# A hand-written opening in another order, and a full 128-row sample chunk in the HGRN tail

## The chip, the core and the metric

The kernel runs on one core of a Trainium2 chip, in one launch. The metric is the device time of that core in microseconds (us), the median of several runs; smaller is better. A core has five engines that each take their instructions strictly in order: TensorE (PE, matmuls; its weight loads are shown apart as PEld), VectorE (DVE), ScalarE (ACT), GpSimd (POOL), and SyncE (SP), which here only issues the transfers (DMA). They wait for each other through semaphores.

## What is computed

One inference step of one layer: 2048 new tokens of one stream (the prompt) and 64 tokens of a running stream (the sample), 1024 columns each, in float32.

```python
h = rms_norm(x, norm_g);  proj = h @ w_in                     # 6656 columns
hg_q, hg_f, hg_i, hg_gate, rt_q, rt_k, rt_v, rt_gate, xa_q, xa_gate = split(proj)
o_hg, s_hg = hgrn2_chunkwise(silu(hg_q), (1-lb)*sigmoid(-hg_f), hg_i, log f, state)   # 8 heads of 128
o_rt, s_rt = retention_chunkwise(rope(rt_q), rope(rt_k), rt_v, state)                 # 4 heads
m = rms_norm(mem, mem_norm_g);  mk, mv = m @ w_mem_k, m @ w_mem_v                      # 256 memory rows
o_xa = softmax(xa_q @ mk.T) @ mv                                                       # 4 heads
mixed = concat(norm(o_hg)*silu(hg_gate), norm(o_rt)*silu(rt_gate), o_xa*silu(xa_gate))
y = rms_norm(x + mixed @ w_out)                                # and the new states, mk and mv are outputs
```

The sample uses its own memory keys and values and its own states.

## The kernel before

**Matmuls.** Every large product is made of three matmuls in a 32-bit format of PE: each operand is split into a high part (ACT casts, L240 `split`, L379) and a low part (DVE subtracts, L241, L381), and hi*hi, lo*hi and hi*lo are summed in one PSUM bank. `gemm_col` (L243) makes 128 columns of a projection for one tile of tokens: 8 steps of the 1024 rows with 3 matmuls each, 24 in all. `gemm_pair` (L258) makes two such columns at once, step by step in turn, 48 matmuls.

**Weights.** All weights go through one list (`wsrc`) of 0.5 MB pieces in the order of their use: 4 pieces of `w_mk`, 4 of `w_mv`, then `w_in` and `w_out`. A piece is loaded to one of three staging tiles (`wst`), split to one of six pairs `whi`, `wlo`, and its staging tile is free again when DVE's part is done; only then can SP issue the load that reuses it. `w_rel` gives credit for the next split.

**Order.** PE's and SP's orders, and in the opening also those of ACT, DVE and POOL, are those of the code (`manual_schedule`). SP's transfers rotate over eight completion semaphores, so a transfer also waits for the eighth one ahead of it. After the opening, short tasks (`task`, `poll`) are put between the columns' steps at times that a running sum of estimated PE time (`pe`) sets; the `D_` constants are their delays.

**The opening.** From the start on:
- The memory (256 rows, transposed) is scaled and split to `mh` (L882 on ACT, L883 on DVE). POOL squares and sums it (L885, L887).
- The four memory-key heads (`gemm_col` on `mh`), then the memory values from four weight pieces of 256 rows (L942, called mv here).
- The row scales: squares summed over the 1024 columns, a matmul with ones (`rs_tok`, L335), DVE's scale and offset (L342) and POOL's power -0.5 (L343). To use them along the free axis, they are put on a diagonal (`rs_diag`, L349), broadcast by a matmul with ones (`rs_bcast`, L357) and copied by ACT (L361). This is done for the memory, for tile 0 (tokens 0 to 511) and tile 1 (512 to 1023).
- `h_split` then scales each of the eight row groups of a tile (L378) and splits it to `ha` (tile 0) or `hb` (tile 1). Between the steps of tile 0, `sq1` squares tile 1 on ACT and sums it on POOL (L929, L931).
- `gemm_pair` of the first two retention-gate columns for tile 0 (PE, 43 to 63 us), two more columns, and the same for tile 1.

**The HGRN tail.** Tokens come in chunks of 128; the last tile (1792, 320 tokens) has two prompt chunks and the sample's 64 rows. For each of 8 heads and each tile, `hgrn_tail` transposes the keys (L526), makes the scores as matmuls of 32 output rows each (L533), masks them (L538), makes the state products (L542), the outputs from scores and from state (L574, L577), squares and normalises them (L582, L236, L237, L586) and transposes them back (L593). The sample's chunk has L = 64: its steps use 64 rows, and `parts` splits the shared steps in two.

## Time and profile before

| | |
|---|---|
| median of 3 runs | 1966.73 us (1966.49 to 1967.02) |
| the profiled execution: its time | 1968.01 us |
| its span (first to last instruction) | 1966.2 us |
| PE busy | 1924.1 us, 98% |
| DVE, ACT, POOL busy | 1049.2, 584.6, 163.9 us |
| mean granted PE clock | 0.992 |
| transfers | 153.19 MB, mean 78 GB/s |

In the rows of this document a line number (L249) is that of the kernel's file, an arrow reads "out from in", xN is a count, and a row in order of time begins with its start and its length in us; what stands in brackets is the idle time of the engine before it and what ended that. Names are those of the code without buffer numbers. [...]

### The profile page before, as it was taken

The page shows a single profiled execution, that of the slowest core. Times are in us where ns is not written, and L with a number is a line of the kernel's source. Part 1 is how long each engine was busy: PE and PEld are TensorE (multiplying, and loading weights), DVE is VectorE, ACT ScalarE, POOL GpSimd, SP SyncE. Part 2 cuts the span into 40 slices and gives each one's busy share as a digit, 9 for nine tenths or more (in the row PEclk, how much of TensorE's full clock was granted, in tenths as well). Part 3 has the DMA queues.
Part 4 walks back from the last instruction along what each step waited for, and adds up shares of the span by engine and source line. Part 5 has one row for each costly group of instructions (what it writes and reads, how often), then busy time and mean ns, then how long its engine had stood idle before and what let it go on. Part 6 is the DMA issues. An engine that isn't in the chain of part 4 may idle for free.

```text
span 1966.2 us, 28106 instructions
## 1 busy us (share of the span) xinstructions
PE 1924.1 (98%) x10906; PEld 1624.0 (83%) x10906; DVE 1049.2 (53%) x2511; ACT 584.6 (30%) x1418; POOL 163.9 (8%) x363
## 2 busy tenths in 40 slices
PE   8999999999999999999999999999999999999998
PEld 7788788888888788987788888888888978888886
DVE  7616647762767547417637775477765642222222
ACT  5522223322223534412323332233334431111111
POOL 3100101000100100000101111021100000000000
PEclk8999999999999999999999999999999999999999
DMA  7422311111111423311311111111222352223321
GB/s 251 146 67 63 87 50 48 60 54 49 44 44 60 130 75 121 124 53 53 91 46 49 49 49 48 43 49 49 59 70 70 106 160 86 86 89 109 102 70 59
DMA packets 116741, 153.19 MB, mean 78 GB/s; under 512 B 13312, under 2 KB 79232, under 8 KB 116608
## 3 DMA queue, kind: packets, MB, share of 16 engines
q1 hardware_dynamic: 116608, 151.41, 25.2%
q8 instruction: 85, 1.39, 0.3%
q14 instruction: 48, 0.39, 0.1%
HBM read 117.69 MB, written 33.69 MB: 77 GB/s over the span
## 4 chain that ended last, share of the span: by engine, by line
PE 87%; DVE 6%; DMA 3%; ACT 2%; issue 1%; POOL 1%; SPq 0%; DVEq 0%; POOLq 0%; ACTq 0%
PE acc L249 39%; PE acc L1131 19%; PE acc L294 15%; PE scb L533 2%; PE ob L542 2%; PE ob L574 2%; PE ob L577 1%; PE acc L806 1%; PE ob L762 1%; DVE wlo L241 1%; PE acc L264 1%; PE tr L593 1%; PE tr L526 1%; PE tr L784 1%; DMA wst<-w_mv_t 1%
## 5 line engine op out<-in xcount | busy, mean ns | idle before, releaser
L249 PE MATMUL acc<-hb,whi 128*128 128x320 f32 (+2 forms) x1728 | 414.6, 330 | 0.4 <-DVE hb L381 0.4
L249 PE MATMUL acc<-ha,whi 128*128 128x512 f32 x1120 | 354.6, 398 | 0.0
L249 PEld LDWEIGHTS acc<-hb,whi 128*128 128x128 f32 x1728 | 289.3, 189 | 25.0 <-issue 4.4
L241 DVE TENSOR_TENSOR wlo<-wst,whi 128x1024 fp32r<-128x1024 f32 x118 | 146.0, 1246 | 273.4 <-ACT whi L240 272.4
L249 PE MATMUL acc<-hb,wlo 128*128 128x320 f32 (+2 forms) x864 | 281.3, 326 | 0.0
L249 PEld LDWEIGHTS acc<-ha,whi 128*128 128x128 f32 x1120 | 204.3, 188 | 42.9 <-issue 2.4
L249 PE MATMUL acc<-ha,wlo 128*128 128x512 f32 x560 | 219.4, 392 | 0.0
L240 ACT CAST whi<-wst 128x1024 fp32r<-128x1024 f32 x118 | 122.9, 1050 | 225.4 <-PE acc L249 172.1
L249 PEld LDWEIGHTS acc<-hb,wlo 128*128 128x128 f32 x864 | 163.1, 189 | 11.1
L294 PE MATMUL acc<-whi,ha 128*128 128x512 f32 x512 | 161.2, 396 | 0.0
L294 PE MATMUL acc<-whi,hb 128*128 128x512 f32 x512 | 160.1, 394 | 0.0
L1131 PE MATMUL acc<-whi,s 128*128 128x512 f32 x396 | 125.9, 396 | 1.3 <-ACT s L240 1.0
L249 PEld LDWEIGHTS acc<-ha,wlo 128*128 128x128 f32 x560 | 105.4, 188 | 23.1
L294 PEld LDWEIGHTS acc<-whi,hb 128*128 128x128 f32 x512 | 94.5, 188 | 19.9 <-issue 1.2
L294 PEld LDWEIGHTS acc<-whi,ha 128*128 128x128 f32 x512 | 93.8, 188 | 19.9 <-issue 1.2
L294 PE MATMUL acc<-wlo,ha 128*128 128x512 f32 x256 | 100.1, 391 | 0.0
L294 PE MATMUL acc<-wlo,hb 128*128 128x512 f32 x256 | 99.8, 390 | 0.0
L1131 PE MATMUL acc<-hb,s 128*128 128x512 f32 x400 | 98.5, 403 | 0.0
L1131 PE MATMUL acc<-ha,s 128*128 128x512 f32 x400 | 96.4, 396 | 0.0
L1131 PEld LDWEIGHTS acc<-hb,s 128*128 128x128 f32 x400 | 76.9, 192 | 18.7
L241 DVE TENSOR_TENSOR s<-mst,s 128x512 fp32r<-128x512 f32 (+1 forms) x64 | 40.5, 672 | 96.4 <-ACT s L240 96.4
L1131 PEld LDWEIGHTS acc<-whi,s 128*128 128x128 f32 x396 | 74.3, 188 | 19.6 <-ACT s L240 1.3
(236 smaller groups left out, 2932.0 us busy)
## 6 DMA issues: line engine op xcount, KB each, us to landing
wst<-w_in_t SPq DMA_DIRECT2D x104, 512.0 KB, 3.9
mixT<-s SPq DMA_DIRECT2D x64, 256.0 KB, 3.7
mst<-mixT SPq DMA_DIRECT2D x30, 512.0 KB, 6.0
wst<-w_out_t SPq DMA_DIRECT2D x16, 512.0 KB, 3.9
xq<-x_prompt SPq DMA_DIRECT2D x18, 256.0 KB, 5.4
o_yp<-xq SPq DMA_DIRECT2D x18, 256.0 KB, 2.1
s<-mixT SPq DMA_DIRECT2D x16, 256.0 KB, 3.0
s<-x_prompt SPq DMA_DIRECT2D x16, 256.0 KB, 5.0
```

The lines of the kernel that those rows point to most:

```text
L240: S.copy(hi, src)
L241: V.tensor_tensor(out=lo, in0=src, in1=hi.bitcast(F32), op=ALU.subtract)
L249: T.matmul(ps[:, 0:nt], w[a][:, kk, :], ht[b][:, kk, 0:nt], start=(n == 0), stop=(n == 23))
L264: T.matmul(ps[:, 0:nt], w[a][:, kk, :], ht[b][:, kk, 0:nt], start=(kk == 0 and a + b == 0), stop=(kk == KT - 1 and a == 1))
L294: T.matmul(ps[0:L, :], ht[b][:, kk, o:o + L], w[a][:, kk % 2, :], start=(n == 0), stop=(n == 23))
L526: T.transpose(trk[0:L, c * 128:(c + 1) * 128], kch[:, c * 128:c * 128 + L], ident)
L533: T.matmul(scb[32 * e:32 * e + 32, c * 128 + 32 * e:c * 128 + L], K[:, c * 128 + 32 * e:c * 128 + 32 * e + 32], Qe[:, c, E_OFF[e]:E_OFF[e] ...
L542: T.matmul(db[:, c * 128:(c + 1) * 128], kT[0:L, c * 128:(c + 1) * 128], vt[c][0:L], start=True, stop=True)
L574: T.matmul(ob[0:L, c * 128:(c + 1) * 128], A[0:L, c * 128:c * 128 + L], vt[c][0:L], start=True, stop=first)
L577: T.matmul(ob[0:L, c * 128:(c + 1) * 128], qst[:, c * 128:c * 128 + L], st[c][0], start=False, stop=True)
L593: T.transpose(tro[:, o:o + L], on[0:L, c * 128:(c + 1) * 128], ident[0:L, 0:L])
L1131: T.matmul(ps, m[a][:, kk % 4], w[b], start=(n == 0), stop=(n == 16 * len(terms) - 1))
```

## The change

It has two parts. The changed file's line numbers are lower or higher by some tens: L516, L522, L531, L563, L566 and L581 are there what L526, L533, L542, L574, L577 and L593 are here, L368 and L371 are L378 and L381, L896 and L897 are L882 and L883, L933 is L942, and L858 is the new sum of squares.

1. **The opening is written in another order.** SP issues the memory ahead of all but the first weight piece, and tile 0 before the value weights. The squares of the memory are made by ACT and all sums by DVE (`add_tree`), also those of tiles 0 and 1; POOL keeps the power. ACT makes the squares of tile 0 before the memory-key heads end. The row scale of tile 0 is made right after these heads. The memory-key results stay in two PSUM banks; their scale, their stores and the mask are made by a task (`mk_fin`) some 24 us of PE time later. One value-weight quarter of the four is done at a time between the other steps, the last two after the broadcast. Tile 1's sums are made after tile 0's splits, and its scale is delayed further (`D_PQ1`, `D_PR1`).
2. **The sample's chunk in `hgrn_tail` has 128 rows**, the lower 64 being zero or masked: POOL fills the lower half of its value tile with zeros, the score matmuls go over four groups of 32 rows instead of two, and the steps split by `parts` are one step each.

On POOL, at the start of its work (in both, behind the fills of constants; `rsall` are the row scales, `s` working tiles). Before:

```order
L885 ISA
L885 TENSOR_TENSOR s<-s 128x512 x2
L887 TENSOR_TENSOR s<-s 128x512
L885 TENSOR_TENSOR s<-s 128x512
L887 TENSOR_TENSOR s<-s 128x512
L885 TENSOR_TENSOR s<-s 128x512
L887 TENSOR_TENSOR s<-s 128x512
L343 TENSOR_TENSOR rsall<-rsall,nhalf 128x2
L371 TENSOR_TENSOR s<-s 128x512
L343 TENSOR_TENSOR rsall<-rsall,nhalf 128x4
L931 TENSOR_TENSOR s<-s 128x512 x7
```

Now:

```order
L343 ISA
L343 TENSOR_TENSOR rsall<-rsall,nhalf 128x4
L343 TENSOR_TENSOR rsall<-rsall,nhalf 128x2
L343 TENSOR_TENSOR rsall<-rsall,nhalf 128x4
L236 TENSOR_SCALAR rs_1311<-ss_1305 128x4
```

All squares and sums have left POOL; of the opening it keeps three powers.

On DVE, where tile 0 is scaled and split (`s_230` and the even numbers after it are the row groups of tile 0, `wst_250` and `wst_339` the two weights of the first `gemm_pair`). Before:

```order
L241 TENSOR_TENSOR wlo_461<-wst_250,whi_460 128x1024
L349 TENSOR_SCALAR s_466<-cst_103,rsall_142 128x128 x4
L241 TENSOR_TENSOR wlo_472<-wst_339,whi_471 128x1024
L378 SCALAR_TENSOR_TENSOR s_230<-s_230,cols_101,s_494 128x512
L378 SCALAR_TENSOR_TENSOR s_232<-s_232,cols_101,s_494 128x512
L381 TENSOR_TENSOR ha1_428<-s_230,ha0_427 128x512
L378 SCALAR_TENSOR_TENSOR s_234<-s_234,cols_101,s_494 128x512
L381 TENSOR_TENSOR ha1_428<-s_232,ha0_427 128x512
L241 TENSOR_TENSOR wlo_513<-wst_345,whi_512 128x1024
```

Now (`s_172` to `s_178`, then `s_186` on are tile 0, `wst_359` is the last value weight, `wst_373` and `wst_398` are the pair's):

```order
L241 TENSOR_TENSOR wlo_457<-wst_359,whi_456 128x1024
L368 SCALAR_TENSOR_TENSOR s_174<-s_174,cols_101,s_405 128x512
L371 TENSOR_TENSOR ha1_453<-s_172,ha0_452 128x512
L368 SCALAR_TENSOR_TENSOR s_176<-s_176,cols_101,s_405 128x512
L371 TENSOR_TENSOR ha1_453<-s_174,ha0_452 128x512
L241 TENSOR_TENSOR wlo_483<-wst_373,whi_482 128x1024
L368 SCALAR_TENSOR_TENSOR s_178<-s_178,cols_101,s_405 128x512
L371 TENSOR_TENSOR ha1_453<-s_176,ha0_452 128x512
L342 TENSOR_SCALAR rsall_142<-tr_435 128x2
L368 SCALAR_TENSOR_TENSOR s_186<-s_186,cols_101,s_405 128x512
L371 TENSOR_TENSOR ha1_453<-s_178,ha0_452 128x512
L241 TENSOR_TENSOR wlo_501<-wst_398,whi_500 128x1024
```

The pair's weights stood ahead of the first scaled group; they now stand behind three and five of them.

On PE, the outputs of one HGRN head of the last tile (`v` values, `abuf` masked scores, `Sc`, `Sn`, `Ss` states). Before:

```order
L249 MATMUL acc<-ha_6307,wlo 128x512
L574 MATMUL ob<-v,abuf_109 128x128
L577 MATMUL ob<-Sc,s 128x128
L574 MATMUL ob<-v,abuf_109 128x128
L577 MATMUL ob<-Sn,s 128x128
L574 MATMUL ob<-v,abuf_109 64x128
L577 MATMUL ob<-Ss,s 64x128
L249 MATMUL acc<-ha_6307,whi 128x512
```

Now:

```order
L249 MATMUL acc<-ha_6298,wlo 128x512
L563 MATMUL ob<-v,abuf_109 128x128
L566 MATMUL ob<-Sc,s 128x128
L563 MATMUL ob<-v,abuf_109 128x128
L566 MATMUL ob<-Sn,s 128x128
L563 MATMUL ob<-v,abuf_109 128x128
L566 MATMUL ob<-Ss,s 128x128
L249 MATMUL acc<-ha_6298,whi 128x512
```

The places are the same; the third chunk's two matmuls now have 128 rows like the others.

The core of the diff:

```diff
-D_PQ1 = 4.0
-K_W0 = 2
-K_W1 = 5
-I_TK = 1
-I_BC = 2
+D_PR1 = 3.5
+D_PQ1 = 8.5
+D_MK0 = 24.0
+D_MK1 = 3.0
+D_MK2 = 8.0
...
-    def sq_sum(sts, n):
-        sqs = []
...
-            e.tensor_tensor(out=sqs[a][:, 0:n], in0=sqs[a][:, 0:n], in1=sqs[b][:, 0:n], op=ALU.add)
-        return sqs[0:1]
...
-        yield D_PR
+        yield D_PR if sts is None else D_PR1
...
-        for c, (o, L) in enumerate(subs):
-            T.transpose(trk[0:L, c * 128:(c + 1) * 128], kch[:, c * 128:c * 128 + L], ident)
+        for c in range(nch):
+            T.transpose(trk[:, c * 128:(c + 1) * 128], kch[:, c * 128:(c + 1) * 128], ident)
             pe(0.107)
         kT = slot()
-        for Lp, c0, c1 in parts(subs):
-            S.copy(kT[0:Lp, c0 * 128:c1 * 128], trk[0:Lp, c0 * 128:c1 * 128])
-        for c, (o, L) in enumerate(subs):
-            for e in range(L // 32):
-                T.matmul(scb[32 * e:32 * e + 32, c * 128 + 32 * e:c * 128 + L], K[:, c * 128 + 32 * e:c * 128 + 32 * e + 32],
-                         Qe[:, c, E_OFF[e]:E_OFF[e] + L - 32 * e], start=True, stop=True, tile_position=(0, 32 * e))
-                pe((L - 32 * e) / 600.0)
+        S.copy(kT[:, 0:ntp], trk[:, 0:ntp])
+        for c in range(nch):
+            for e in range(4):
+                T.matmul(scb[32 * e:32 * e + 32, c * 128 + 32 * e:(c + 1) * 128], K[:, c * 128 + 32 * e:c * 128 + 32 * e + 32],
+                         Qe[:, c, E_OFF[e]:E_OFF[e] + 128 - 32 * e], start=True, stop=True, tile_position=(0, 32 * e))
+                pe((128 - 32 * e) / 600.0)
...
-        for c, (o, L) in enumerate(subs):
-            T.matmul(db[:, c * 128:(c + 1) * 128], kT[0:L, c * 128:(c + 1) * 128], vt[c][0:L], start=True, stop=True)
+        for c in range(nch):
+            T.matmul(db[:, c * 128:(c + 1) * 128], kT[:, c * 128:(c + 1) * 128], vt[c], start=True, stop=True)
             pe(0.213)
...
-        for c, (o, L) in enumerate(subs):
+        for c in range(nch):
             first = st[c][0] is None
-            T.matmul(ob[0:L, c * 128:(c + 1) * 128], A[0:L, c * 128:c * 128 + L], vt[c][0:L], start=True, stop=first)
+            T.matmul(ob[:, c * 128:(c + 1) * 128], A[:, c * 128:(c + 1) * 128], vt[c], start=True, stop=first)
             pe(0.213)
             if not first:
-                T.matmul(ob[0:L, c * 128:(c + 1) * 128], qst[:, c * 128:c * 128 + L], st[c][0], start=False, stop=True)
+                T.matmul(ob[:, c * 128:(c + 1) * 128], qst[:, c * 128:(c + 1) * 128], st[c][0], start=False, stop=True)
...
         on = kT
-        for c, (o, L) in enumerate(subs):
-            S.activation(on[0:L, c * 128:(c + 1) * 128], ob[0:L, c * 128:(c + 1) * 128], AF.Square, accum_out=ss[0:L, c:c + 1])
+        for c in range(nch):
+            S.activation(on[:, c * 128:(c + 1) * 128], ob[:, c * 128:(c + 1) * 128], AF.Square, accum_out=ss[:, c:c + 1])
         rs = small(4, "rs4")
-        for Lp, c0, c1 in parts(subs):
-            rsqrt_small(rs[0:Lp, c0:c1], ss[0:Lp, c0:c1], c1 - c0, 1.0 / 128, 4 * EPS)
-            V.tensor_tensor(
-                out=on[0:Lp, c0 * 128:c1 * 128].rearrange("p (c w) -> p c w", w=128),
-                in0=ob[0:Lp, c0 * 128:c1 * 128].rearrange("p (c w) -> p c w", w=128),
-                in1=bc(rs[0:Lp, c0:c1].rearrange("p (c o) -> p c o", o=1), [Lp, c1 - c0, 128]), op=ALU.mult)
+        rsqrt_small(rs[:, 0:nch], ss[:, 0:nch], nch, 1.0 / 128, 4 * EPS)
+        V.tensor_tensor(
+            out=on[:, 0:ntp].rearrange("p (c w) -> p c w", w=128),
+            in0=ob[:, 0:ntp].rearrange("p (c w) -> p c w", w=128),
+            in1=bc(rs[:, 0:nch].rearrange("p (c o) -> p c o", o=1), [P, nch, 128]), op=ALU.mult)
         yield D_HG3
         tro = trp()
-        for c, (o, L) in enumerate(subs):
-            T.transpose(tro[:, o:o + L], on[0:L, c * 128:(c + 1) * 128], ident[0:L, 0:L])
+        for c in range(nch):
+            T.transpose(tro[:, c * 128:(c + 1) * 128], on[:, c * 128:(c + 1) * 128], ident)
...
-    wpos["credit"] = 1
-    w_pump()
-    mtot = None
+    def w_one():
+        wpos["credit"] += 1
+        w_pump()
+
+    def add_tree(sqs, pairs):
+        for a, b in pairs:
+            V.tensor_tensor(out=sqs[a], in0=sqs[a], in1=sqs[b], op=ALU.add)
+
+    def square(src, dst=None):
+        dst = dst if dst is not None else slot()
+        S.activation(dst, src, AF.Square)
+        return dst
+
+    def rs_sum(rsp, tots, n):
+        for i in range(n):
+            for j, tot in enumerate(tots):
+                T.matmul(rsp[:, i:i + 1], tot[:, i * 128:(i + 1) * 128], ones[:, 0:1], start=(j == 0), stop=(j == len(tots) - 1))
+                pe(0.107)
+
+    wpos["ahead"] = 0
+    w_fetch(1)
+    mem = []
     for k0 in range(0, KT, 2):
         st = slot()
         dma(st.rearrange("p (k n) -> p k n", k=2), io["memT"][k0 * 128:(k0 + 2) * 128].rearrange("(k p) n -> p k n", p=P))
-        for j in range(2):
-            x, g = st[:, j * 256:(j + 1) * 256], mg[:, k0 + j:k0 + j + 1]
...
+    w_fetch(3)
+    xs0 = []
+
+    def x0_load(k):
+        x = slot()
+        dma(x, io["xT"][k * 128:(k + 1) * 128, 0:512])
+        xs0.append(x)
+
+    for k in range(4):
+        x0_load(k)
+    wpos["ahead"] = 3
+    w_one()
+    for k in range(4, KT):
+        x0_load(k)
     dma(cst, io["cst"])
-    wpos["credit"] = 5
-    wpos["ahead"] = 0
-    w_pump()
-    xT0 = io["xT"][:, 0:512]
-    xs0 = []
     for k in range(KT):
...
+        x, g = mem[k // 2][:, k % 2 * 256:(k % 2 + 1) * 256], mg[:, k:k + 1]
+        hi, lo = mh[0][:, k, 0:NMEM], mh[1][:, k, 0:NMEM]
+        S.activation(hi, x, AF.Copy, scale=g)
+        V.scalar_tensor_tensor(out=lo, in0=x, scalar=g, in1=hi.bitcast(F32), op0=ALU.mult, op1=ALU.subtract)
+    mks = [obank(), obank()]
+
+    def mk(h):
+        gemm_col(w_get(1)[0], mh, NMEM, False, mks[h // 2][:, h % 2 * 256:(h % 2 + 1) * 256])
+
+    w_one()
+    mk(0)
+    w_one()
+    mk(1)
+    mk2 = w_get(1)[0]
+    sqs = [square(x) for x in xs0[0:4]]
+    add_tree(sqs, ((0, 1), (2, 3), (0, 2)))
+    w_one()
+    sqs += [square(x) for x in xs0[4:8]]
+    add_tree(sqs, ((4, 5), (0, 4), (6, 7), (0, 6)))
+    gemm_col(mk2, mh, NMEM, False, mks[1][:, 0:256])
+    gemm_col(w_get(1)[0], mh, NMEM, False, mks[1][:, 256:512])
+    rsp = trp()
+    rs_sum(rsp, sqs[0:1], 4)
+    w_one()
+    for st in mem:
+        square(st, st)
+    add_tree(mem, ((0, 1),))
+    rs_fin(rsp, 4, 0)
+    add_tree(mem, ((2, 3),))
...
     mps = [acc(), scb]
...
+    def mv(i):
         w = wt[ws[i]]
...
                 for a, b in ((0, 0), (0, 1), (1, 0)):
                     T.matmul(mps[m], mh[b][:, kk, m * 128:(m + 1) * 128], w[a][:, j, :], start=(kk == 0 and a + b == 0), stop=(kk == 7 and a == 1))
                     pe(512 / 2400.0)
-        if i == I_TK:
-            rs_tok(xt0, [128] * 4, 0)
-            w_rel()
-            dg0 = rs_diag([128] * 4, 0)
-            w_rel()
-        if i == I_BC:
-            bc0 = rs_bcast(dg0, [128] * 4)
-            for kk in h_split(h0, xs0, bc0, 512):
-                if kk < KT:
-                    sq1(kk)
-    w_rel()
-    w_rel()
+
+    mv(0)
+    dg0 = rs_diag([128] * 4, 0)
+    add_tree(mem, ((0, 2),))
+    w_one()
+    bc0 = rs_bcast(dg0, [128] * 4)
+    xs1 = []
+    for k in range(KT):
+        x = vpool.tile([P, 512], F32, tag="v", name="x1")
+        dma(x, io["xT"][k * 128:(k + 1) * 128, 512:1024])
+        xs1.append(x)
+    mv(1)
+    rsm = trp()
+    rs_sum(rsm, [mem[0][:, 0:256], mem[0][:, 256:512]], 2)
+    mv(2)
+    h0 = h_tile("a")
+    hmap[0, 0], hdone[0, 0] = h0, [True]
+    sq1 = []
+    for kk in h_split(h0, xs0, bc0, 512):
+        if kk in (0, 2, 4):
+            w_one()
+        if kk == 0:
+            mv(3)
+        if kk == 3:
+            rs_fin(rsm, 2, 17)
+        if kk:
+            sq1.append(square(xs1[kk - 1]))
...
-    prep_tile(0, 1, D_HS0, xs1, xsum, D_PQ1)
+    add_tree(sq1, ((0, 1), (2, 3), (0, 2), (4, 5), (0, 4), (6, 7), (0, 6)))
+    w_one()
+    w_one()
+    prep_tile(0, 1, D_HS0, xs1, sq1[0:1], D_PQ1)
...
-    maskf = slot()
-    dma(maskf, io["mask"])
-    V.tensor_copy(mask, maskf)
+    w_rel()
+    w_rel()
...
+    def mk_fin():
+        yield D_MK0
+        dgm = rs_diag([128, 128], 17)
+        yield D_MK1
+        mbc = rs_bcast(dgm, [128, 128])
+        for h in range(0, 4, 2):
+            kv = slot()
+            V.tensor_tensor(out=kv.rearrange("p (a n) -> p a n", a=2), in0=mks[h // 2].rearrange("p (a n) -> p a n", a=2),
+                            in1=bc(mbc[:, 0:NMEM].rearrange("p (a n) -> p a n", a=1), [P, 2, NMEM]), op=ALU.mult)
+            for j in range(2):
+                store(mkd[h + j], kv[:, j * 256:(j + 1) * 256])
+                store(io["o_mkT"][h + j], kv[:, j * 256:(j + 1) * 256])
+        maskf = slot()
+        dma(maskf, io["mask"])
+        yield D_MK2
+        V.tensor_copy(mask, maskf)
+
+    task(None, mk_fin(), 0)
...
                         fold(v[0:L], ps)
+                        G.memset(v[L:P], 0.0)
```

More of the change, by code (lines that the diff above doesn't have):

```diff
@@ L596, in hgrn_tail @@
         store(mixT[h * 128:(h + 1) * 128, tok0:tok0 + nt], gs[:, 0:nt])
-    def parts(subs):
-        full = sum(1 for _, L in subs if L == 128)
-        out = []
-        if full:
-            out.append((128, 0, full))
-        if full < len(subs):
-            out.append((DEC, full, len(subs)))
-        return out
     def retention(ws, ht, tok0, nt, vt, R, dtab, last_tile):
@@ L878, in layer_kernel @@
         dma(st.rearrange("p (k n) -> p k n", k=2), io["memT"][k0 * 128:(k0 + 2) * 128].rearrange("(k p) n -> p k n", p=P))
-        for j in range(2):
-            x, g = st[:, j * 256:(j + 1) * 256], mg[:, k0 + j:k0 + j + 1]
-            hi, lo = mh[0][:, k0 + j, 0:NMEM], mh[1][:, k0 + j, 0:NMEM]
-            S.activation(hi, x, AF.Copy, scale=g)
-            V.scalar_tensor_tensor(out=lo, in0=x, scalar=g, in1=hi.bitcast(F32), op0=ALU.mult, op1=ALU.subtract)
-        sq = slot()
-        G.tensor_tensor(out=sq, in0=st, in1=st, op=ALU.mult)
@@ L886, in layer_kernel @@
-        if mtot is not None:
-            G.tensor_tensor(out=sq, in0=sq, in1=mtot, op=ALU.add)
-        mtot = sq
-    dma(cst, io["cst"])
-    wpos["credit"] = 5
-    wpos["ahead"] = 0
-    w_pump()
-    xT0 = io["xT"][:, 0:512]
-    xs0 = []
-    for k in range(KT):
-        x = slot()
-        dma(x, xT0[k * 128:(k + 1) * 128])
-        xs0.append(x)
-    wpos["ahead"] = 3
-    w_fetch()
-    mks = []
-    for h in range(4):
-        mks.append(gemm_col(w_get(1)[0], mh, NMEM, False, obank() if h < 2 else None))
-        if h == 1:
-            rs_tok([mtot[:, j * 256:(j + 1) * 256] for j in range(2)], [128, 128], 17)
-            dgm = rs_diag([128, 128], 17)
-            xt0 = sq_sum(xs0, 512)
-            w_rel()
-            w_rel()
@@ L910, in layer_kernel @@
-    mbc = rs_bcast(dgm, [128, 128])
-    for h in range(4):
-        kv = slot()
-        V.tensor_tensor(out=kv[:, 0:NMEM], in0=mks[h][:, 0:NMEM], in1=mbc[:, 0:NMEM], op=ALU.mult)
-        store(mkd[h], kv[:, 0:NMEM])
-        store(io["o_mkT"][h], kv[:, 0:NMEM])
-    xs1 = []
-    for k in range(KT):
-        x = vpool.tile([P, 512], F32, tag="v", name="x1")
-        dma(x, io["xT"][k * 128:(k + 1) * 128, 512:1024])
-        xs1.append(x)
+        mem.append(st)
+    w_fetch(3)
+    xs0 = []
@@ L921, in layer_kernel @@
+    rsp = trp()
[7 more added lines that the diff above has]
+    w_one()
     ws = w_get(4)
     mps = [acc(), scb]
-    h0 = h_tile("a")
-    hmap[0, 0], hdone[0, 0] = h0, [True]
-    xsum = []
-    def sq1(k):
-        sq = slot()
-        S.activation(sq, xs1[k], AF.Square)
-        if xsum:
-            G.tensor_tensor(out=sq, in0=sq, in1=xsum.pop(), op=ALU.add)
-        xsum.append(sq)
-        if k in (K_W0, K_W1):
-            w_rel()
@@ L936, in layer_kernel @@
-    for i in range(4):
+    def mv(i):
         w = wt[ws[i]]
```

9 lines of the change are left out of this document (1 added, 8 removed).

## The prediction

> **What bounds the kernel now.** I read the page first (busy time by engine), then the table of busy time by stage, the list of what TensorE (PE) waited for, its rows in order of time, and the chain of work that ended last. The page:
>
> ```profile
> span 1966.2 us, 28106 instructions
> PE 1924.1 (98%) x10906; PEld 1624.0 (83%) x10906; DVE 1049.2 (53%) x2511; ACT 584.6 (30%) x1418; POOL 163.9 (8%) x363
> ```
>
> PE is the bound: what shortens PE's own row of work, or takes away one of its few waits, shortens the run; the rest is hidden. Three stages by the stage table (PE, PEld, VectorE (DVE), ScalarE (ACT), GpSimd (POOL), then the granted PE clock):
>
> ```profile
> 8.00:17.00 9.00, 6.11 (x22) 4.34 (x22) 9.00 (x9) 5.45 (x10) 7.79 (x7) 0.62 0.42 161
> 48.00:63.50 15.50, 10.63 (x39) 8.00 (x40) 14.94 (x15) 10.54 (x17) 8.10 (x5) 0.89 0.25 73
> 1020.00:1500.00 480.00, 477.87 (x3382) 424.84 (x3381) 325.82 (x992) 148.21 (x387) 61.46 (x164) 1.00 0.18 52
> ```
>
> In the opening (first two rows) DVE is full and PE is not; the clock that PE is granted also falls after slack, which costs 9.0 x 0.38 = 3.4 us and 15.5 x 0.11 = 1.7 us. In the third row, which holds the HGRN heads with the sample chunk, PE has 2.1 us free in 480: each 0.1 us that PE works less there is 0.1 us of the run.
>
> ```profile
> PE acc L264 <- DVE ha L381: 6.6, 3, 3.1
> ...
> 22.55 0.48 PE L249 MATMUL acc<-hb,whi 128*128 128x256 f32 x2
> ...
> 28.38 0.60 PE L357 MATMUL tr<-s,ones 128*128 128x128 f32 x4
> ...
> 43.05 0.74 PE L264 MATMUL acc<-ha,whi 128*128 128x512 f32 x2
> ...
> 63.15 0.95 PE L335 MATMUL tr<-ones,s 128*128 128x1 f32 x8
> ```
>
> The last two memory-key heads, 48 matmuls at full clock, take 28.38 - 22.55 = 5.8 us, 2.9 a head. The first pair of projection columns (`gemm_pair`) runs from 43.05 to 63.15, 20.1 us. The next pair, of tile 1, shows what 48 such matmuls cost when nothing is late, in the chain's rows:
>
> ```profile
> 63.31 0.78 PE tr L335 x8
> ...
> 66.29 0.89 PE tr L357 x8
> ...
> 76.04 10.88 PE acc L264 x48
> 86.92 10.88 PE acc L249 x48
> ```
>
> So the first pair loses 9.2 us, 6.6 of them to waits for DVE's splits. The second pair ends at 86.92, from where PE has no wait for over 100 us: that is the end of the opening, and I count its gain there.
>
> **The opening, step by step.** Prices, by source line, by groups and by time (a 128x512 DVE step starts 0.67 us after the one before it), then GB/s in 40 slices of the first 130 us, and the time to landing of tile 1's loads:
>
> ```profile
> L883 DVE SCALAR_TENSOR_TENSOR hb<-s,cols,hb x8: 474/1257/1495, 7.8 to 16.2; 128x256 fp32r<-128x256 f32 x8
> L241 DVE TENSOR_TENSOR wlo<-wst,whi 128x1024 fp32r<-128x1024 f32 x118 | 146.0, 1246 | 273.4 <-ACT whi L240 272.4
> L240 ACT CAST whi<-wst 128x1024 fp32r<-128x1024 f32 x14 | 14.4, 1042 | 15.7 <-DMA wst<-w_mv_t 10.5 <-DMA wst<-w_in_t 2.9 <-DMA wst<-w_mk_t 2.1
> L381 DVE TENSOR_TENSOR ha<-s,ha 128x512 fp32r<-128x512 f32 x8 | 7.5, 932 | 0.1
> 73.56 0.75 DVE L378 SCALAR_TENSOR_TENSOR x<-x,cols,s 128x512 f32<-128x512 f32 x1
> 74.23 0.69 DVE L381 TENSOR_TENSOR hb<-x,hb 128x512 fp32r<-128x512 f32 x1
> 64.38 1.02 POOL L343 TENSOR_TENSOR rsall<-rsall,nhalf 128x4 f32<-128x4 f32 x1 [2.78 <-DVE rsall L342]
> 65.43 0.88 DVE L349 TENSOR_SCALAR s<-cst,rsall 128x128 f32<-128x128 f32 x4 [1.13 <-POOL rsall L343]
> GB/s 70 355 379 233 0 57 299 311 401 369 40 279 295 400 299 166 0 78 86 106 294 374 396 40 164 5 0 142 180 97 226 227 96 5 0 0 0 0 0 0
> x<-xT SPq DMA_DIRECT2D x8, 256.0 KB, 6.8
> ```
>
> 1. *Memory splits.* The eight low-part steps of `mh` (L883) take 0.47 us once and 1.26 in the median, and POOL is busy 7.79 of the 9 us beside them with the memory squares. The change gives POOL none of these (squares go to ACT, sums to DVE), so I take 0.47 each: from 7.3 (the memory loads are issued one 0.5 MB load earlier) to 11.1 instead of 16.7. The same holds later for L381 (0.93 us beside POOL, 0.69 alone).
> 2. *Memory-key heads.* PE follows these steps through head 0. The next two weights are split by DVE at 12.3 and 13.6 (1.25 each), so heads 1 and 2 run back to back, 2.9 each, to 18.1. Head 3's weights are load 13 in SP's queue, 4.2 MB with all ahead of it: at some 0.39 MB a us (the full slices show 355 to 401 GB/s) from 2.7 us on, and near 1 us to complete, landed by 14.5, cast and split by 16.8: hidden. Heads end at 21.0.
> 3. *Row scale of tile 0.* The sum matmuls (0.78), L342, POOL's power (1.02) give 23.0; DVE then first splits the second value weight. ACT casts it behind the first one (landed near 18.7, after 6.0 MB) and four memory squares: 18.7 + 1.04 + 2.4 + 1.04 = 23.2, with hand-overs 23.3, so its split ends at 24.6. Four diagonal scales (0.88): 25.5; broadcast (0.89) and ACT's copy (0.6): 27.0. On PE one value-weight quarter (mv) covers most of this.
> 4. *Up to the second weight of the pair.* Before that split DVE's queue now holds five scale and four low-part steps (9 x 0.67 = 6.0) and three weight splits (3.75). It waits three times for ACT, which casts the scaled tile (0.6, estimated as half of the 1.04 plus its fixed part) and then the weight (1.04): 1.65 the first time, some 1.0 each after that. POOL's power of the memory rows may block one step, 0.5. Sum 13.9: the split is done at 40.9.
> 5. *The pair.* Its weights used to be split first and `ha` came late; now `ha` is early and the second weight is what comes late next. PE has ended mv at about 35, does three matmuls, and waits from 36.5 to 40.9; then 45 x 0.227 = 10.2 us, to 51.1. A wait of 4.4 us is longer than those after which the clock fell in the trace, where it cost 1.7 and 3.4 us; I take 2.5, between them: the pair ends at 53.6 instead of 63.2, a gain of 9.6.
> 6. *Tile 1.* Its scales now start later after the pair. From the pair's end: sums after six of eight steps of the third column (4.1), 0.78, then on DVE power 1.02, diagonal 0.88, a weight split and a gate step (1.9): 8.7. PE reaches the broadcast at 9.0; 0.89 and 0.6 make 10.5, three scales 2.0 and a low part 0.67: 13.2, for a second pair that could start 76.04 - 63.15 = 12.9 after the first ends. Some 0.5 lost with semaphores.
>
> The bounds of the opening: no loss of clock and a wait of 2 us, gain 13; a chain 3 us longer and twice the clock's loss, gain 4.
>
> At nothing I cost the rest: seven POOL sums become seven DVE steps (4.7 us) between the pair and the next splits, under 10 us of PE work; the key scale, its eight stores and the mask go to later tasks, where SP and DVE have room (DVE 53% busy; the second pair does not need them, the keys are first read in the last HGRN head); the late broadcast is the same matmuls at another place. If DVE were the bound there, its three steps of some 0.7 us would show.
>
> **The sample chunk.** The tile of 320 tokens has two full chunks and one of 64 rows. One head of it (left alone: starts of PE rows, and the row after each group), and then a head with four full chunks:
>
> ```profile
> 1063.56 0.74 PE L533 MATMUL scb<-Qe,s 128*32 128x128 f32 x20
> ...
> 1066.41 1.02 PE L542 MATMUL ob<-v,s 128*128 128x128 f32 x6
> 1067.36 0.76 PE L249 MATMUL acc<-ha,whi 128*128 128x512 f32 x2
> ...
> 1070.72 0.39 PE L574 MATMUL ob<-v,abuf 128*128 128x128 f32 x2
> 1070.94 0.39 PE L577 MATMUL ob<-Sn,s 128*128 128x128 f32 x2
> 1071.26 0.43 PE L574 MATMUL ob<-v,abuf 64*64 64x128 f32 x2
> 1071.62 0.43 PE L577 MATMUL ob<-Ss,s 128*64 128x128 f32 x2
> 1071.98 0.73 PE L249 MATMUL acc<-ha,whi 128*128 128x512 f32 x2
> ...
> 1076.90 0.58 PE L593 MATMUL tr<-cst,s 128*128 128x128 f32 x3
> 1077.41 0.73 PE L249 MATMUL acc<-ha,whi 128*128 128x512 f32 x2
> ...
> 1080.15 1.06 PE L533 MATMUL scb<-Qe,s 128*32 128x128 f32 x32
> ...
> 1083.05 1.05 PE L542 MATMUL ob<-v,s 128*128 128x128 f32 x8
> 1083.85 0.48 PE L249 MATMUL acc<-hb,whi 128*128 128x256 f32 x2
> ...
> 1092.71 0.60 PE L593 MATMUL tr<-cst,s 128*128 128x128 f32 x4
> 1093.07 0.53 PE L249 MATMUL acc<-hb,whi 128*128 128x320 f32 x2
> ```
>
> PE pays for the change of shape. State products (L542): 0.95 us for three chunks with a part one, 0.80 for four full, so 0.60 for three: -0.35. Outputs (L574, L577): a full one 0.22; the three steps around the part chunk take 0.32, 0.36, 0.36: -0.38. Transposes (L593): 0.51 for three, 0.36 for four, so 0.27: -0.24. Against it come two more score matmuls and two wider ones (L533): 12 instructions more take 0.32 longer, so four more +0.11. Together -0.86 a head, eight heads: -6.9 us. I take -7.0, as the matmuls after the group also start sooner. ACT's, POOL's and DVE's second steps fall away; they lie under PE's work but in one place:
>
> ```profile
> 1455.24 0.96 PE L762 MATMUL ob<-s 128*128 128x256 f32 x6 [2.13 <-DVE s L586]
> ```
>
> After the last head PE waits for the two normalising steps to free a bank; one instead of two, -0.4. The two POOL fills of the value tile's lower half are under PE's work.
>
> [...]
>
> **Sum.** -9.6 + 0.5 - 7.0 - 0.4 = -16.5 us. Against the profiled execution: span 1966.2 to 1949.7. Its own time is 1968.01, 1.3 above the median of the three runs, 1966.73; the median I forecast is 1950.2.
>
> **Rivals.**
> - *Half of the opening's gain.* Tile 1's loads are issued from 28 us on, and ACT squares one of them ahead of each of the pair's casts. At the 6.8 us to landing of before the first is there at 34.8, not 32.5: DVE's second weight comes 2.3 us later, and another 2 us of half clock follow. Opening -4.8; 1954.5. For it: ACT waits 10.5 us for w_mv loads before. Against: the loads now follow each other without gaps.
> - *A shorter wait.* The splits end by 39 and the clock holds: opening -12; 1947.3. Against: five ACT-DVE hand-overs have to fit.
> - *The 64-row chunk was not what cost.* The 0.36 is the state's load or a bank change and stays at 128 rows: 8 x 0.11 = 0.9 us lost instead of 7.0 gained, 1958.1. Against: four-chunk heads change states and banks too and show 0.22. [...]
> - *Slower.* Tile 1's split becomes the bound: DVE has seven sums and four weight splits before its first scale. It decides from 17 us of delay of the second pair on (0.5 in my sum); at 21, 1970.7. The rows above put its first low part at 13.2 after the pair, so this is far.
> - *No difference.* The opening gains under 4 us in all and the chunk nothing.
>
> **Chances.** The forecast 0.64 (its own range 1946.5 to 1953.5, from the bounds of the opening and 0.7 to 1.0 us a head), half the opening 0.15, shorter wait 0.08, chunk without gain 0.08, no difference 0.03, slower 0.02. The range from 1946.3 to 1956.0 takes in the first two and leaves out the chunk's rival and the outer part of the third. Of a run of this kernel 0.2% (3.9 us) can be told from no change: faster 0.95, same 0.03, slower 0.02.
>
> **What would show it.** L883's successor at 0.47 to 0.6 us a step; POOL with three steps in the opening; the pair's first wait for `wlo`, not `ha`, 3 to 5 us long; its end near 53 and that of the second pair near 78; in the sample tile 0.22 between output matmuls and 0.6 for the state products. I am wrong if ACT waits for DMA between 28 and 40, if the clock stays low after 50, or if the sample tile's steps keep 0.36.

## The result, and the profile after

The changed kernel takes 1949.73 us (median of 4 runs, 1948.53 to 1950.56) against 1966.61 for the kernel before beside it: 16.9 us less, a ratio of 0.9917 (95% interval 0.9900 to 0.9934). 1950.2 us and 16.5 us less were forecast. The profiled execution took 1948.53 us, with a span of 1946.7. Line numbers below are those of the changed kernel unless said otherwise.

The page of the changed kernel, then two places in its chain of waits (start, length, what): the second pair (L264) and the start of the token-major products (L294), which is a common place behind the opening; its row in the kernel before stands last.

```profile
span 1946.7 us, 28118 instructions
PE 1912.0 (98%) x10938; PEld 1620.4 (83%) x10938; DVE 1043.7 (54%) x2512; ACT 586.5 (30%) x1414; POOL 140.6 (7%) x335
...
68.02 10.95 PE acc L264 x47
...
90.31 55.76 PE acc L294 x246
```

```profile
97.80 55.76 PE acc L294 x246
```

PE is still 98% busy. 7.5 us of the gain lie ahead of L294, 1.6 us less than forecast in this execution. The opening's rows in order of time: the memory splits as one line of the source view (minimum, median and maximum in ns, first and last start), POOL's powers, then the second weight of the pair (ACT's cast, DVE's low part), and PE.

```profile
L897 DVE SCALAR_TENSOR_TENSOR hb<-s,cols,hb x8: 480/484/486, 7.0 to 9.8; 128x256 fp32r<-128x256 f32 x8
24.06 1.03 POOL L343 TENSOR_TENSOR rsall<-rsall,nhalf 128x4 f32<-128x4 f32 x1 [21.60 <-DVE rsall L342]
38.80 1.14 POOL L343 TENSOR_TENSOR rsall<-rsall,nhalf 128x2 f32<-128x2 f32 x1 [13.72 <-DVE rsall L342]
59.80 1.01 POOL L343 TENSOR_TENSOR rsall<-rsall,nhalf 128x4 f32<-128x4 f32 x1 [19.86 <-DVE rsall L342]
...
39.94 1.04 ACT L240 CAST whi<-wst 128x1024 fp32r<-128x1024 f32 x1
41.01 1.23 DVE L241 TENSOR_TENSOR wlo<-wst,whi 128x1024 fp32r<-128x1024 f32 x1 [1.03 <-ACT whi L240]
...
20.77 0.94 PE L868 MATMUL tr<-ones,s 128*128 128x1 f32 x8
37.26 0.62 PE L264 MATMUL acc<-ha,whi 128*128 128x512 f32 x2
41.03 1.22 PE L264 MATMUL acc<-ha,whi 128*128 128x512 f32 x2 [2.93 <-ACT whi L240]
54.49 0.61 PE L249 MATMUL acc<-ha,whi 128*128 128x512 f32 x2
68.02 0.50 PE L264 MATMUL acc<-hb,whi 128*128 128x512 f32 x1 [0.42 <-DVE hb L371]
```

The memory splits take 0.48 us each, POOL keeps three steps. The key heads end at 20.77 instead of 28.38. PE waits 2.93 us for the pair's second weight (the low part follows at 42.24), and the pair ends at 54.49 instead of 63.15. The stage table (busy time of PE, PEld, DVE, ACT, POOL, then the granted clock) shows what follows the wait: from 40.4 to 47.2 the clock is 0.50.

```profile
8.00:17.00 9.00, 8.03 (x63) 7.62 (x62) 7.40 (x12) 7.77 (x13) 0.00 (x0) 1.00 1.04 399
37.00:48.00 11.00, 8.04 (x22) 5.58 (x21) 9.88 (x16) 8.10 (x14) 1.14 (x1) 0.69 0.50 176
```

One head with the sample chunk, PE in order of time, and the row behind each group. Rows of PE overlap (a single matmul of 128x128 has a row of 0.28 us, and the next one starts 0.11 us after its start), so the time of a group is read from its start to the start of the row behind it:

```profile
1055.51 0.84 PE L522 MATMUL scb<-Qe,s 128*32 128x128 f32 x24
1056.28 0.73 PE L249 MATMUL acc<-ha,whi 128*128 128x512 f32 x2
...
1058.46 0.83 PE L531 MATMUL ob<-v,s 128*128 128x128 f32 x6
1059.05 0.71 PE L249 MATMUL acc<-ha,whi 128*128 128x512 f32 x2
...
1062.56 0.39 PE L566 MATMUL ob<-Sn,s 128*128 128x128 f32 x2
1062.78 0.39 PE L563 MATMUL ob<-v,abuf 128*128 128x128 f32 x2
1063.01 0.39 PE L566 MATMUL ob<-Ss,s 128*128 128x128 f32 x2
1063.15 0.71 PE L249 MATMUL acc<-ha,whi 128*128 128x512 f32 x2
...
1068.01 0.49 PE L581 MATMUL tr<-cst,s 128*128 128x128 f32 x3
1068.26 0.71 PE L249 MATMUL acc<-ha,whi 128*128 128x512 f32 x2
```

State products 0.59 us (0.95 before), the last three output steps 0.22, 0.23 and 0.14 (0.32, 0.36, 0.36), transposes 0.25 (0.51), scores 0.77 (0.67). The eight heads with the sample alternate with those of the tiles at 1024 and 1536. From the first column of this stretch to the end of the wait behind its last head PE takes 431.5 us instead of 440.1: 8.65 us for eight heads.

### The profile page after: what moved, and what is told of

It is laid out like the page before. It is cut to its first block, busy times and chain, and to the rows that moved or that the text cites. A ratio compares the mean times of both kernels' runs of the same rounds, so it can differ in the third digit from the quotient of the medians.

```text
span 1946.7 us, 28118 instructions
## 1 busy us (share of the span) xinstructions
PE 1912.0 (98%) x10938; PEld 1620.4 (83%) x10938; DVE 1043.7 (54%) x2512; ACT 586.5 (30%) x1414; POOL 140.6 (7%) x335
## 4 chain that ended last, share of the span: by engine, by line
PE 88%; DVE 5%; DMA 2%; ACT 2%; issue 1%; POOL 1%; SPq 0%; DVEq 0%; POOLq 0%; ACTq 0%
PE acc L249 39%; PE acc L1159 19%; PE acc L294 16%; PE scb L522 2%; PE ob L531 2%; PE ob L563 1%; PE ob L566 1%; PE acc L264 1%; PE acc L785 1%; PE ob L741 1%; DVE wlo L241 1%; PE tr L516 1%; PE tr L763 1%; PE tr L581 1%; POOL rs L237 0%
## 5 line engine op out<-in xcount | busy, mean ns | idle before, releaser
L249 PE MATMUL acc<-hb,wlo 128*128 128x256 f32 (+2 forms) x848 | 277.7, 327 | 0.0
L294 PE MATMUL acc<-whi,ha 128*128 128x512 f32 x512 | 161.5, 397 | 0.0
L294 PE MATMUL acc<-whi,hb 128*128 128x512 f32 x512 | 160.0, 394 | 0.0
L294 PEld LDWEIGHTS acc<-whi,hb 128*128 128x128 f32 x512 | 94.5, 188 | 19.8 <-issue 1.2
L294 PEld LDWEIGHTS acc<-whi,ha 128*128 128x128 f32 x512 | 94.1, 189 | 19.6 <-issue 1.3
L294 PE MATMUL acc<-wlo,ha 128*128 128x512 f32 x256 | 100.1, 391 | 0.0
L294 PE MATMUL acc<-wlo,hb 128*128 128x512 f32 x256 | 99.8, 390 | 0.0
L241 DVE TENSOR_TENSOR s<-mst,s 128x512 fp32r<-128x512 f32 (+1 forms) x64 | 40.4, 672 | 97.2 <-ACT s L240 97.2
L1159 PEld LDWEIGHTS acc<-ha,s 128*128 128x128 f32 x400 | 75.0, 188 | 18.2
```

What stands on the lines that cost most here:

```text
L241: V.tensor_tensor(out=lo, in0=src, in1=hi.bitcast(F32), op=ALU.subtract)
L249: T.matmul(ps[:, 0:nt], w[a][:, kk, :], ht[b][:, kk, 0:nt], start=(n == 0), stop=(n == 23))
L294: T.matmul(ps[0:L, :], ht[b][:, kk, o:o + L], w[a][:, kk % 2, :], start=(n == 0), stop=(n == 23))
L1159: T.matmul(ps, m[a][:, kk % 4], w[b], start=(n == 0), stop=(n == 16 * len(terms) - 1))
```

## The experiments

The table collects from the profiles: the start of L294; the stretch of HGRN heads that holds the sample's eight, from its first column to the end of the 2.13 us wait behind its last head; whether the clock fell behind that wait; PE's last wait ahead of the final products. Ratios and medians are each against the kernel before on the same chip (1966.62, 1967.07 and 1966.20 us for e1 to e4, e5 to e8, e9 to e11); e5, e6 and e7 have a single time each.

| kernel | L294 | heads | clock fell | last wait | median us | ratio |
|---|---|---|---|---|---|---|
| before | 97.80 | 440.1 | no | 2.25 | 1966.61 | |
| changed | 90.31 | 431.5 | yes | 1.33 | 1949.73 | 0.9917 |
| e1_tail_only | 97.72 | 431.5 | yes | 1.27 | 1958.15 | 0.9956 |
| e2_open_only | 89.68 | 440.1 | no | 2.21 | 1956.87 | 0.9946 |
| e3_pool_squares | 92.48 | 431.5 | yes | 2.68 | 1952.66 | 0.9927 |
| e4_early | 83.80 | 431.5 | yes | 2.37 | 1944.24 | 0.9881 |
| e5_all_64 | 87.90 | 434.5 | no | 1.12 | 1949.66 | |
| e6_old_delays | 87.80 | 431.5 | yes | 1.92 | 1947.74 | |
| e7_key_early | 89.56 | 431.5 | no | 1.94 | 1948.00 | |
| e8_same | 88.68 | 431.5 | yes | 1.12 | 1946.95 | 0.9898 |
| e9_early2 | 85.78 | 431.5 | no | 1.13 | 1944.06 | 0.9889 |
| e10_early_again | 83.25 | 431.5 | yes | 1.29 | 1942.59 | 0.9883 |
| e11_changed | 88.37 | 431.5 | yes | 2.26 | 1948.91 | 0.9910 |

**The two parts alone: e1_tail_only and e2_open_only.** e1 has the part of the diff in `hgrn_tail` and the fill of the value tile, e2 the rest:

```diff
e1:  -        for c, (o, L) in enumerate(subs):          (old opening kept)
     +        for c in range(nch):
     +                        G.memset(v[L:P], 0.0)
e2:  +    w_fetch(1)                                     (old hgrn_tail kept)
     +    mem = []
```

> The kernel before with the 128-row sample chunk alone, the opening as it was. By the prediction's terms (7.0 in the steps, 0.4 in the last wait) 1966.6 - 7.4 = 1959.2 us. By the changed kernel's trace the tile with the sample is 7.4 us shorter (474.6 to 467.2 between the same two places) and the last wait is still 2.13 us, so the same number by another split. Rival: the output stage, 4.1 us shorter in the profile of the changed kernel (a wait of 1.33 instead of 2.25 us and no stretch of lower clock after it), owes that to the chunk: then 1955 to 1957. Rival: the chunk and the opening do not add up, and the chunk alone gives under 5 us.

> The kernel before with the new opening alone, the sample chunk with 64 rows as before. By the prediction's terms (-9.6 and +0.5) 1957.5 us. By the changed kernel's trace, in which the first common place behind the opening (start of the token-major products) comes 7.5 us earlier, 1959.1. Rival: the output stage's 4.1 us belong to the opening (everything behind it runs some 8 us earlier against the clock's windows): then 1955 to 1957.

e1 gained 8.5 us (interval of the ratio 0.9940 to 0.9972: 5.5 to 11.8 us), e2 9.75 (0.9933 to 0.9960: 7.9 to 13.2). The sum, 18.2, agrees with the whole, 16.9 to 20.1, within the intervals. In the trace the terms are separate: e1 has the old start of L294 (97.72) and the new time of the heads (431.5), e2 the new start and the old time of the heads. (What the expectations of e2 and e8 call the clock's windows is seen in the traces as stretches of 3.41 us at whose edges the granted clock changed: last section. The 7.4 us that e1's expectation quotes are these 8.65 less the 1.25 that the clock's fall behind the wait takes back.) The output stage follows neither part: its last wait, 1.12 to 2.68 us over all profiles, was 1.33, 1.12 and 2.26 in three profiles of the changed kernel itself.

**POOL beside DVE: e3_pool_squares.** The memory's squares and sums go back to POOL:

```diff
+    for st in mem:
+        sq = slot()
+        G.tensor_tensor(out=sq, in0=st, in1=st, op=ALU.mult)
...
-    for st in mem:
-        square(st, st)
-    add_tree(mem, ((0, 1),))
```

> The changed kernel with one part undone: the squares and sums of the memory are made by POOL again, during the splits of the memory; ACT loses four squares (2.2 us) and DVE three sums (2.0 us) that stood between 22 and 28 us. If POOL's work beside them is what slowed the low-part steps, they go from 0.47 us or less back to about 1.26 each, 6 us in all, the memory-key heads end 4 to 6 us later than 20.8, and the run is 2 to 5 us slower than the changed kernel. Rival: POOL does not slow them (the old 1.26 came from late loads): the steps stay near 0.45 us, the relief of ACT and DVE moves the tile's scale up to 2 us forward, and the run is the same or up to 2 us faster.

The same line of the source view, and the start of L294:

```profile
L897 DVE SCALAR_TENSOR_TENSOR hb<-s,cols,hb x8: 473/1256/1496, 7.6 to 15.8; 128x256 fp32r<-128x256 f32 x8
...
92.48 55.76 PE acc L294 x246
```

The median step goes from 484 back to 1256 ns, its largest to 1496, as in the kernel before (1257 and 1495). Up to the end of the splits only POOL's work is different; what ACT and DVE lose lies behind them. The splits end 6 us later and the heads at 26.45 instead of 20.77, but the first pair starts only 2.9 us later (40.13 instead of 37.26): ACT's and DVE's relief lies between, so this run shows what slowed the splits, but not what POOL's squares alone cost the run. L294 starts 2.2 us later than in the first profile of the changed kernel and 3.5 later than in the mean of the five profiles with its opening (89.0). The median is 2.9 us above the first of the changed kernel, which is from another set of runs; the intervals of the two ratios overlap.

**What the pair waits for: e4_early, again as e10_early_again, beside e11_changed.** Cast and low part of three weights become separate steps. With them the last value-weight quarter, the memory's scale and tile 1's squares move one or two row groups back (not shown):

```diff
+    late = w_hi()
     for kk in h_split(h0, xs0, bc0, 512):
-        if kk in (0, 2, 4):
-            w_one()
+        if kk in (1, 2, 3):
+            w_lo(*late)
+        if kk in (1, 2):
+            late = w_hi()
```

> The changed kernel with another place for three weight splits: the casts of the last value weight and of the pair's two weights stand ahead of the first, third and fourth scaled row group on ACT, and their low parts on DVE behind the second, third and fourth, instead of the whole splits behind groups 1, 3 and 5. If the second weight is what the pair waited for (2.9 us, then 6 us at half clock), it is split by 36 to 37 us, the pair runs from 37.3 without a long wait and ends between 48 and 50 instead of 54.5: 4 to 6 us faster than the changed kernel, 1944 to 1946 us. Rival: the row groups then come late and PE waits for them instead, in small pieces: 0 to 2 us faster. Rival: the pair's weights have not landed by 32 to 34 us: ACT stands still for them and nothing is gained. Rival: tile 1's scales become the bound and take the gain back: the second pair still starts at 67 to 68 us.

> e4_early again, beside the changed kernel on the same chip. If the pair's late weight was the bound of the opening, it is 4 to 7 us faster than the changed kernel here too (6.5 us at the place behind the opening in the first pair of profiles, 90.31 and 83.80; 4.9 against the changed kernel's best profile, 88.68).

> The changed kernel beside them, for a ratio on one chip: 1947 to 1950 us. The clock's part in the two places, 37 to 47 us in the opening and behind the wait of 2.13 us after the last HGRN head, should follow from where the wait lies: a fall in the next 3.41 us if nearly all of the 2.13 us lie between two changes of the clock's 3.41 us raster, none if they are split.

DVE and PE in e4, the second weight's low part and the first pair:

```profile
35.35 1.22 DVE L867 TENSOR_TENSOR wlo<-wst,whi 128x1024 fp32r<-128x1024 f32 x1
...
36.41 0.62 PE L264 MATMUL acc<-ha,whi 128*128 128x512 f32 x2
47.30 0.61 PE L249 MATMUL acc<-ha,whi 128*128 128x512 f32 x2
...
83.80 55.77 PE acc L294 x246
```

The weight is split by 36.6, and the pair takes 10.89 us, as long as the second pair took before. DVE does the same steps; what went is its waiting for ACT's casts, which now stand one row group ahead of the low parts. Beside each other on one chip the version takes 1942.59 us and the changed kernel 1948.91: 6.3 less, of which 5.1 lie ahead of L294 (83.25 and 88.37). It is the fastest version run: 0.9883 of the kernel before (0.9868 to 0.9898). All three rivals fell.

**One step more: e9_early2.**

```diff
+    w_one()
     add_tree(sq1, ((0, 1), (2, 3), (0, 2), (4, 5), (0, 4), (6, 7), (0, 6)))
     w_one()
-    w_one()
```

> The version e4_early with one split more moved: the weight of the third column is split ahead of tile 1's seven sums instead of behind them. In e4_early PE waited 0.34 us for it (48.24) and then 0.43 us at the second pair; the sums ended at 47.0 and PE's matmul on them stood at 52.0. If there is room, the 0.34 goes and nothing else moves: 0.3 us, less than can be told. If the sums come too late by the 1.2 us, the wait appears at their matmul instead.

The second case came true. PE waits at tile 1's sums instead, and the clock falls behind that:

```profile
52.31 0.91 PE L335 MATMUL tr<-ones,s 128*128 128x1 f32 x7 [1.31 <-DVE s L873]
54.40:57.80 3.40, 3.40 (x9) 2.65 (x8) 2.50 (x7) 1.17 (x2) 1.13 (x1) 0.50 0.82 288
...
85.78 55.76 PE acc L294 x246
```

0.31 us saved became 2.5 lost at L294. The median (1944.06, against 1942.59) is too near to tell the two apart; the trace does.

**Tile 1's delays and the key scale: e6_old_delays and e7_key_early.**

```diff
e6:  -D_PR1 = 3.5      e7:  -D_MK0 = 24.0
     +D_PR1 = 1.5           +D_MK0 = 1.0
     -D_PQ1 = 8.5           -D_MK1 = 3.0
     +D_PQ1 = 4.0           +D_MK1 = 1.5
```

> The changed kernel with the old delays of tile 1's scale (sums' matmul and broadcast stand right behind the pair, one column earlier). The prediction's sixth step took tile 1 for just late (0.5 us), bound by the chain from the sums to the first low part; the trace of the changed kernel shows 0.42 us of wait at the second pair and the first low part done at 68.0. If the delays set that place, the first low part is done by 62 to 64 us, the 0.42 us wait goes, and PE waits instead up to 2 us at the broadcast, which now stands ahead of its operands: the common place behind the opening (90.31) moves between -0.5 and +1.5 us. If the chain itself was the bound, nothing moves.

> The changed kernel with the memory-key scale (a broadcast of two matmuls, two DVE steps, eight stores, the mask) right behind the first pair instead of 24 us of PE work later. The prediction costs the postponement at nothing. If DVE has room there, the place behind the opening stays at 90.3 within 0.3 us. Rival: the two steps of 0.65 us and two diagonals of 0.28 us stand ahead of tile 1's splits on DVE, the second pair's first wait grows from 0.42 to about 2 us, and the place moves 1 to 2 us back: then the postponement is a part of the gain.

From the end of the first pair to L294 the changed kernel takes 35.82 us (35.83 in e8_same), e6 35.88, e7 36.37. In e6 the first low parts are done by 61, and the 0.42 us wait has only moved to the broadcast:

```profile
55.55 1.13 PE L357 MATMUL tr<-s,ones 128*128 128x128 f32 x8 [0.51 <-DVE s L349]
```

So the delays trade one wait for another, and the chain itself is not the bound at the pair. In e7 DVE scales the keys between tile 1's steps, and the postponement is worth 0.5 us, between the two expectations.

**Rows or shape: e5_all_64.** In the tile with the sample the state products use 64 rows in all three chunks, which leaves out half the keys there:

```diff
-            T.matmul(db[:, c * 128:(c + 1) * 128], kT[:, c * 128:(c + 1) * 128], vt[c], start=True, stop=True)
+            R = DEC if subs[-1][1] == DEC else P
+            T.matmul(db[:, c * 128:(c + 1) * 128], kT[0:R, c * 128:(c + 1) * 128], vt[c][0:R], start=True, stop=True)
```

> The changed kernel, but in the tile with the sample the state products (one matmul group of three chunks) use only 64 of the 128 rows in all three chunks; half the keys of the two prompt chunks are left out there. Before, this group took 0.95 us with one 64-row chunk of three, now 0.59 with none. If it is the change of shape that costs (the first matmul of another shape starts 0.21 instead of 0.11 us after the one ahead, and so does the one behind the last), three chunks of 64 rows cost as much as one: 0.85 to 0.95 us. If each 64-row matmul cannot have its weights loaded beside the matmul ahead of it, all six pay: 0.16 to 0.2 us each, 1.0 to 1.3 us. [...]

PE and its weight loads (PEld) around the group:

```profile
1058.10 0.39 PE L249 MATMUL acc<-ha,wlo 128*128 128x512 f32 x1
1058.41 0.74 PEld L532 LDWEIGHTS ob<-v,s 64*128 64x128 f32 x6 [0.35 <-issue]
1058.42 0.93 PE L532 MATMUL ob<-v,s 64*128 64x128 f32 x6
1059.28 0.30 PEld L249 LDWEIGHTS acc<-ha,whi 128*128 128x128 f32 x2
1059.28 0.73 PE L249 MATMUL acc<-ha,whi 128*128 128x512 f32 x2
```

Six matmuls of 64 rows take 0.86 us, and the matmul ahead of them 0.32 instead of 0.23: 0.95 in all, what the group cost before with one such chunk of three. The price is that of two changes of shape: the matmul ahead takes 0.1 longer, the next matmul follows the first of the six after 0.21 instead of 0.11, and the one behind the last after 0.20 instead of 0.03. At the change the weight load starts with its matmul (1058.41 and 1058.42) and not beside the one ahead. It is neither rows nor each matmul: between the changes the matmuls of 64 rows follow each other after 0.11 us, as those of 128 rows do. The outputs and the transposes were not tried in this way; that theirs is the same price is an inference.

**The changed kernel again: e8_same.** Nothing is edited.

> The changed kernel once more, timed in five rounds, for a closer ratio and another profile. Median 1949 to 1951 us. Its opening and the tile with the sample should repeat to 0.5 us (common place behind the opening near 90.3; sample tile 474.6 to 467.2). The output stage may not: in the first profile it was 4.1 us shorter than before, with a wait of 1.33 us and full clock behind it; if that is chance of the clock's windows and of a transfer, it now takes up to 3 us longer.

The time of the heads and the wait repeat to 0.01 us, the opening does not: 88.68 instead of 90.31. The median, 1946.95, is below the expected 1949 to 1951. The output stage was not longer here: from the wait of 1.03 us ahead of it (1558.39 in the first profile) to the end it took 388.1 us, as in the first profile (388.3). In e11_changed, where its last wait was 2.26 us, it took 392.3, and e4_early and e10_early_again, one version, have 392.4 and 389.8.

## Why the prediction was right, and where its steps were off

**The opening: the sum was right, its parts less so.** Forecast -9.1 us at the second pair's end. Five profiles with this opening unchanged (changed, e2, e5, e8, e11) give L294 at 90.31, 89.68, 87.90, 88.68 and 88.37, mean 89.0, against 97.80 and 97.72 with the old one: 8.8 us, between 7.4 and 9.9.
- Steps 1 and 2 held: 0.48 us a split, last one done at 10.3 (11.1 forecast), heads to 20.77 (21.0). e3 shows that POOL's squares and sums were the cause of the slow splits. The near 1 us to complete in step 2 was an estimate: in the kernel before, the first weight, 0.55 MB with what is ahead of it, needs until 4.1 from 2.7 us on at 0.39 MB a us, and its cast began at 4.93. In the changed kernel the cast of head 3's weight waited for its landing and began at 15.21 (14.5 forecast).
- Step 3 was early in the first profile: the copy of the broadcast was done at 28.95, not 27.0. The first value weight could be cast only at 20.93 (forecast 18.7), and behind the wait for it PE had a stretch of 3.4 us at half clock, from 23.3 on. In the other four profiles, without that stretch, the copy was done between 26.88 and 27.94.
- Step 4 was right: from the copy on it took 13.3 us in the first profile and 13.6 to 13.7 in the others, 13.9 forecast. The second weight was split at 42.24 in the first profile and at 40.53 to 41.59 in the others, 40.9 forecast. Three waits of DVE for ACT were counted, and 1.64, 1.04 and 1.03 us are in the trace. The 0.5 us by which POOL's power might block a step was an estimate that no run shows: beside that power (38.80, 1.14 us) DVE's steps took 0.74 and 0.68 us, as behind it.
- Step 5 named the right weight and mis-sized both terms. The wait was 2.9 to 3.1 us instead of 4.4: it began at 36.2 to 38.1 (36.5 forecast), as the value products, of whose four quarters three stand behind the broadcast, ended 0.2 to 2.3 us later than 35; and it ended with ACT's cast (`whi`, 41.03), where the step and the sign of being right let PE wait for the low part (`wlo`), done 1.2 us later. In e8_same the wait began on time, and this alone is the difference. The clock's loss, put at 2.5, was about 1.7 (e5, e11: one stretch of 3.4 us at half clock) or 3.4 (the others: two). The pair ended at 54.49, 53.84, 52.07, 52.85 and 52.53, in the order above; forecast 53.6. e4 shows the wait and its clock to be worth 5 to 6 us.
- Step 6: forecast +0.5; from the first pair to L294 it is 35.82 instead of 34.65, +1.2 (35.82 to 35.84 in all five). The wait at the second pair is 0.42, the key scale's two matmuls now stand there (0.36), the rest is small. What I costed at nothing, the postponed key scale, saves 0.5 (e7).

**The sample chunk was mis-sized low.** Forecast -7.0, measured -8.65. By groups of PE rows over the stretch the state products gave 2.9 (2.8 forecast), the transposes 1.9 (1.9), the scores cost 0.86 (0.9). The outputs gave 3.6 instead of 3.0: the matmul behind them also starts 0.14 instead of 0.36 us after the last one. And 1.0 us lies in the projection columns ahead of these groups, which I had not counted: a matmul ahead of a change of shape took 0.1 us longer.

**The last wait stayed, -0.4 was wrong.** POOL's powers behind the last head before, then the one power and PE's wait now:

```profile
1453.28 0.70 POOL L237 TENSOR_TENSOR rs<-rs,nhalf 128x2 f32<-128x2 f32 x1
1454.23 0.55 POOL L237 TENSOR_TENSOR rs<-rs,nhalf 64x1 f32<-64x1 f32 x1
```

```profile
1437.03 0.85 POOL L237 TENSOR_TENSOR rs<-rs,nhalf 128x3 f32<-128x3 f32 x1
1438.53 0.98 PE L741 MATMUL ob<-s 128*128 128x256 f32 x6 [2.13 <-DVE s L574]
```

One power over three columns takes 0.85 us and one normalising step 0.56, where the second of two steps was 0.55 and 0.28 behind a first that overlapped ACT's squares; these squares now begin 0.34 us after the PE row behind the outputs, not 0.17. The wait is 2.13 us in both, and in eight profiles of eleven with the new chunk the clock then fell: 119.9 us to the next wait instead of 118.6 in the kernel before, 1.25 more. In the three others it is 118.3, so the fall itself costs 1.5.

**The rest.** 8.8 and 8.65 make 17.45 us, less 1.25 where the clock falls behind that wait: 16.2, and the medians say 16.9, 17.3 (e11) and 20.1 (e8). That the forecast 16.5 is so near is in part luck: the chunk gave 1.65 more than forecast, and the last wait and the clock behind it 0.4 + 1.25 less. The 20.1 are more than these terms explain. In e8's profiled execution the output stage was 4.3 us shorter than in the profile before, and in the first profile, whose span was 19.5 shorter, 4.1; e11's was as long as before (392.3), so one kernel shows both. With one profile of the kernel before it stays open what its mean is there. Of the rivals, the half opening needs ACT to wait for a transfer between 28 and 40 us, and it waits there only for DVE; the shorter wait needs the clock to hold, and it fell in all five profiles; the slower case needs a second pair 17 us late, and it starts at 67.20 instead of 75.87; the chunk without gain needs 0.36 between output matmuls, and it is 0.22. No difference is ruled out by e1 and e2, each faster than the kernel before beyond its interval.

## What to carry to other kernels

When one engine is the bound and waits only briefly, look at the engine it waits for and at what that one waits for: DVE was the one waited for, and itself stood still three times for ACT's cast of the same split, and casting one step ahead of the subtract was worth 5 to 6 us, over half of what the whole reordering had brought (8.8). Give a short last chunk the shape of the others when its neighbours on PE are of that shape, and price the change of shape (0.37 us a group in e5), not the rows. A wait is worth more than its length where the clock falls behind it (here 1.5 us more behind the 2.13), so compare kernels over several executions, not by one.
